# A two-layer encoder trunk on one core: token sums, unit order and conditioning products rearranged, and two of four weight sums formed by accumulating transfers

## The chip, the cores and the metric

The kernel runs on one core of a Trainium2 chip, in one launch. The metric is the device time of an execution in microseconds (us), lower is better: 1917.07 us in the median of three runs, 1916.01 to 1919.67. The engines are TensorE (PE; PEld is its weight load), VectorE (DVE), ScalarE (ACT), GpSimd (POOL) and SyncE (SP). Each runs its own instructions in the order of the program and waits for semaphores of the others. SP issues nearly all transfers, POOL a few.

## The reference

Two layers on x (512 tokens by 1024 channels), in float32, each a feed-forward half step, a mixer, and a second half step; the norms are scaled and shifted by m, which is a product of the conditioning vector c with w_mod:

```python
cond = jax.nn.silu(c)
for l in range(DEPTH):
    m = (cond @ w_mod[l] + b_mod[l]).reshape(bsz, 3, 3, D_MODEL)
    x = x + 0.5 * m[:, 0, 2][:, None] * swiglu(adaln_in(x, norm_g[l, 0], m, 0),
                                               ffn_w1[l, 0], ffn_w3[l, 0], ffn_w2[l, 0])
    h = adaln_in(x, norm_g[l, 1], m, 1) @ w_in[l]
    ...  # mixer: windowed attention and short convolution, or axial attention and Hyena
    x = x + m[:, 1, 2][:, None] * (mix @ w_out[l])
    x = x + 0.5 * m[:, 2, 2][:, None] * swiglu(adaln_in(x, norm_g[l, 2], m, 2),
                                               ffn_w1[l, 1], ffn_w3[l, 1], ffn_w2[l, 1])

def swiglu(h, w1, w3, w2):
    return (jax.nn.silu(h @ w1) * (h @ w3)) @ w2
```

D_FF is 2752, that is 21 hidden tiles of 128 and one of 64. The relative bias table (rel_table) enters the first layer's attention, and a filter computed from features, three small layers with sines and a Fourier transform enters the second layer's Hyena.

## The kernel before

**Products.** All data are float32. Each operand is split into a high and a low part (split, L203 on ScalarE copies the high part, L204 on VectorE subtracts), and a product is three matmuls of 128 by 128 weights: high by high, high by low, low by high (mm3, L224 to L226). Tokens stand in columns: 512 in one matmul, or two halves of 256.

**Feed-forward.** Each of the four runs over three groups of hidden tiles. In a group, the up part makes SwiGLU outputs into tiles ga, gb, gc, and then the projection (project, L358) makes eight output tiles dt from all of the group's tiles and adds them into x (L362). The weight of a projection's tile is w2a in the first group (8 loads of 384 KB) and w2b in the others (8 of 512 KB each). (0, 0), (0, 2), (1, 0), (1, 2) name the four by layer and place.

**Seven-product units.** In the first feed-forward tiles 5 to 20, in the others 2 to 20 are each a unit (up_seven): w1 and w3 over two halves of the channels and two halves of the tokens are taken as 2 by 2 blocks, and seven products of block sums replace eight (L477, 12 matmuls of 256 columns each, 84 in a unit). There are 73 units. The sums of tokens, T1 to T4, are made once for each feed-forward (token_sums, L409 to L421, from x, the norm's factor and a second pass of ScalarE at L412). The sums of weights are made in each unit by weight_sums: two loads of 512 KB on SP (raw1 and raw3), four VectorE operations of 512 columns (L454, L455, L457, L459) and splits into S1, S2, S3, S4, A11, A12, A22. The other tiles, which need no sums, are computed directly.

**Conditioning.** m is formed by 144 products (gemv): each is a 512 KB load of w_mod on SP (L240), one VectorE product with accumulation (L248), and a read of the accumulator. They are spread over the projections by a rate, so many for each output tile, as far ahead of their use as the rates put them.

**Bias and filter.** rel_bias (L1099, L1105) forms the bias of the first layer's attention by a small matmul, and repeats it through DRAM with a 2 MB transfer on POOL's queue. hyena_filter makes the filter: three matmuls with sines, eight matmuls (L965), a sum of squares (L978), its norm (L992), and a transform with matrices loaded on POOL's queue (dft_hi, dft_lo).

**Order.** The program is written as one sequence; a framework reorders each engine's instructions at build time by its own estimate, and tiles rotate through pools: 4 raw buffers, 5 each of wh and wl, 2 of e3, 16 of h, and 3 + 1 + 2 + 2 banks of PSUM. A load into a buffer is issued when the last reader of its former content is done. The order of a built program is fixed.

## Time and profile before

| | |
|---|---|
| profiled execution, whole | 1918.76 us |
| its span on the core | 1917.0 us |
| median of three runs | 1917.07 us |
| TensorE, VectorE, ScalarE, GpSimd busy | 1845.9, 1565.1, 1012.5, 3.6 us |
| moved by DMA, mean rate | 269.27 MB, 140 GB/s |

The span is the time from the first to the last instruction on the core, and 1.76 us lie around it. Busy times are sums over an engine's instructions; an engine can be busy and still be slowed, since a matmul's time is longer at a lower granted clock. The chain of work is followed back from the last instruction: at each step to what released it. A wait is idle time of an engine in front of an instruction, named after what ended it. The table of stretches gives for each stretch of the span the busy time of each engine, the granted clock of TensorE as a share of full speed, the share of time that the DMA engines worked, and the rate.

### The profile page before, as it was taken

The numbers are of one execution on the slowest core, as the hardware profiler recorded it, in microseconds if no ns is written. First come the engines' busy times: TensorE is split into PE (matmuls) and PEld (weight loads), VectorE is DVE, ScalarE is ACT, GpSimd is POOL, SyncE is SP. The second block draws the span as 40 slices with busy tenths as digits, with TensorE's granted clock in tenths as the row PEclk, the third lists the DMA queues.
The fourth block names the chain that finished last, engine by engine and source line by source line (L and its number), as shares of the span: only waits on it lengthen the run. The fifth ranks groups of instructions, "written<-read, shape, count | busy, mean of one in ns | idle before, by whom it ended". The sixth has DMA issues, their size and how long they took to land.

```text
span 1917.0 us, 30306 instructions
## 1 busy us (share of the span) xinstructions
PE 1845.9 (96%) x11844; PEld 1645.8 (86%) x11844; DVE 1565.1 (82%) x2681; ACT 1012.5 (53%) x1651; POOL 3.6 (0%) x9
## 2 busy tenths in 40 slices
PE   7889999999999999999989999998999999999999
PEld 5659889888888899798988989977887898898997
DVE  8989878878759898888899976877887889686682
ACT  5525435378848345254663533555788366353451
POOL 0000000000000000000000000000000000000000
PEclk9989999999999999999999999998999999999999
DMA  7664643842321644636427362344222322333231
GB/s 273 221 229 167 221 145 102 294 132 94 100 85 64 229 148 152 222 99 220 155 95 242 110 220 66 115 135 148 72 88 99 121 89 75 102 104 117 88 119 59
DMA packets 83658, 269.27 MB, mean 140 GB/s; under 512 B 10024, under 2 KB 13352, under 8 KB 83514
## 3 DMA queue, kind: packets, MB, share of 16 engines
q1 hardware_dynamic: 81898, 263.13, 41.0%
q0 software_dynamic: 1616, 4.20, 0.6%
q8 instruction: 93, 1.52, 0.3%
q14 instruction: 51, 0.42, 0.1%
HBM read 258.88 MB, written 10.50 MB: 141 GB/s over the span
## 4 chain that ended last, share of the span: by engine, by line
PE 73%; DVE 16%; DMA 6%; ACT 3%; issue 1%; SPq 0%; ACTq 0%; DVEq 0%
PE pA L477 29%; PE pC L358 18%; PE pV L477 5%; DVE wl L204 3%; PE pA L358 3%; DMA raw<-w2b 3%; DVE raw L248 2%; PE pC L225 2%; PE pC L226 2%; PE pC L224 2%; ACT wh L203 2%; DMA raw<-w2a 1%; DMA raw<-w_mod 1%; PE pA L789 1%; DVE h L345 1%
## 5 line engine op out<-in xcount | busy, mean ns | idle before, releaser
L203 ACT CAST wh<-raw 128x1024 fp32r<-128x1024 f32 (+2 forms) x393 | 372.8, 951 | 547.4 <-PE pA L477 194.6
L204 DVE TENSOR_TENSOR wl<-raw,wh 128x1024 fp32r<-128x1024 f32 (+2 forms) x393 | 432.1, 1102 | 120.3 <-ACT wh L203 117.1
L477 PE MATMUL pA<-h,wh 128*128 128x256 f32 x1752 | 331.2, 283 | 10.1 <-ACT h L203 9.2
L477 PE MATMUL pA<-e,wh 128*128 128x256 f32 x1752 | 333.4, 288 | 6.8 <-ACT tl L486 3.5
L477 PEld LDWEIGHTS pA<-e,wh 128*128 128x128 f32 x1752 | 271.5, 191 | 22.4 <-ACT tq L493 13.1
L477 PEld LDWEIGHTS pA<-h,wh 128*128 128x128 f32 x1752 | 275.7, 191 | 13.3 <-ACT h L203 9.9
L477 PE MATMUL pA<-e,wl 128*128 128x256 f32 x876 | 246.8, 282 | 0.0
L477 PE MATMUL pA<-h,wl 128*128 128x256 f32 x876 | 244.7, 283 | 1.9 <-DVE wl L204 1.9
L358 PE MATMUL pC<-gb,wh 128*128 128x512 f32 (+1 forms) x800 | 227.3, 368 | 3.6 <-ACT gb L203 1.6
L358 PE MATMUL pC<-ga,wh 128*128 128x512 f32 (+1 forms) x648 | 183.6, 371 | 5.0 <-DVE mod L261 2.6
L248 DVE SCALAR_TENSOR_TENSOR raw<-raw,cond 128x1024 f32<-128x1024 f32 x144 | 174.5, 1221 | 15.8 <-DMA raw<-w_mod 14.8
L358 PEld LDWEIGHTS pC<-gb,wh 128*128 128x128 f32 x800 | 143.9, 189 | 34.8 <-ACT gb L203 3.0
L477 PEld LDWEIGHTS pA<-h,wl 128*128 128x128 f32 x876 | 165.6, 189 | 2.3 <-DVE wl L204 2.3
L477 PEld LDWEIGHTS pA<-e,wl 128*128 128x128 f32 x876 | 167.4, 191 | 0.0
L358 PE MATMUL pC<-gb,wl 128*128 128x512 f32 (+1 forms) x392 | 143.8, 367 | 0.0
L358 PEld LDWEIGHTS pC<-ga,wh 128*128 128x128 f32 x648 | 115.5, 189 | 27.7 <-issue 3.9
L362 DVE SCALAR_TENSOR_TENSOR x<-pC,mod,x 128x512 f32<-128x512 f32 (+1 forms) x108 | 74.2, 687 | 74.7 <-PE pC L358 74.3
L358 PE MATMUL pC<-ga,wl 128*128 128x512 f32 (+1 forms) x300 | 111.6, 372 | 5.2 <-DVE wl L204 5.1
L203 ACT CAST wh<-e 128x1024 fp32r<-128x1024 f32 x73 | 76.8, 1052 | 60.6 <-PE pV L477 26.5
L477 PE MATMUL pV<-h,wh 128*128 128x256 f32 x584 | 107.1, 282 | 0.0
L225 PE MATMUL pA<-h,wh 128*128 128x256 f32 (+1 forms) x301 | 90.7, 310 | 2.1 <-DVE h L345 2.1
L477 PEld LDWEIGHTS pV<-h,wh 128*128 128x128 f32 x584 | 90.3, 190 | 0.0
(309 smaller groups left out, 3608.3 us busy)
## 6 DMA issues: line engine op xcount, KB each, us to landing
raw<-w SPq DMA_DIRECT2D x164, 512.0 KB, 3.5
raw<-w_mod SPq DMA_DIRECT2D x144, 512.0 KB, 4.5
raw<-w2b SPq DMA_DIRECT2D x64, 512.0 KB, 4.1
raw<-w_in SPq DMA_DIRECT2D x36, 512.0 KB, 4.5
raw<-w2a SPq DMA_DIRECT2D x32, 384.0 KB, 3.6
raw<-w_out SPq DMA_DIRECT2D x16, 512.0 KB, 3.4
raw<-w_start SPq DMA_DIRECT2D x8, 512.0 KB, 4.7
xs<-x SPq DMA_DIRECT2D x16, 256.0 KB, 2.0
```

Source lines behind the costliest of these rows:

```text
L203: self.nc.scalar.copy(out=hi, in_=src)
L204: self.nc.vector.tensor_sub(out=lo, in0=src, in1=hi.bitcast(F32))
L224: mm(out, lhsT=wh, rhs=rh, start=start, stop=False)
L225: mm(out, lhsT=wh, rhs=rl, start=False, stop=False)
L226: mm(out, lhsT=wl, rhs=rh, start=False, stop=stop)
L248: nc.vector.scalar_tensor_tensor(out=raw, in0=raw, scalar=1.0, in1=self.cond, op0=ALU.mult, op1=ALU.mult, accum_out=m[:, c : c + 1])
L345: nc.vector.tensor_sub(out=lo[:, c0:c1], in0=hf, in1=hi[:, c0:c1].bitcast(F32))
L358: nc.tensor.matmul(ps, lhsT=lh, rhs=r, start=q == 0, stop=q == len(todo) - 1)
L362: nc.vector.scalar_tensor_tensor(out=x, in0=ps, scalar=gate[dt], in1=x, op0=ALU.mult, op1=ALU.add)
L477: nc.tensor.matmul(out, lhsT=lh, rhs=rr, start=first and n == 0, stop=n == 11, skip_group_check=True)
L789: nc.tensor.transpose(tp[:, c * P : (c + 1) * P], pt[qb][:, o : o + P], self.ident)
```

## The change

- token_sums reads the parts h (high plus low, one addition of 512 columns per tile) and no longer x and the norm's factor. T1 and T2 have the opposite sign, and so has a unit's result, which the tail multiplies by -1. The split of T1 is put off to first_sum.
- In the first feed-forward, token_sums stands after tile 5 and first_sum after tile 7 of the second group, and tiles 5, 6, 7 are computed directly. 70 units are left.
- A unit's A22 and S4 products and its tail (finish) are issued after the next unit's A11 product. The first unit after the token sums has S4 and S1 exchanged (late_t1), and the tail of a group's last unit is done in two halves.
- Of the weight sums, a21 + a22 and a21 + a11 are formed by two transfers on POOL's queue that add 256 KB each into the target in SBUF (accum_op); the first goes into a tile s that a third load on SP of 256 KB fills. The other two stay on VectorE.
- The rates of the conditioning products change, and 24 are placed in units (in_up).
- rel_bias is called at the end of the third group in place of the second; the three small layers of the filter (filter_mlp) one group earlier.

```diff
--- before.py
+++ after.py
@@ -389,36 +389,33 @@
...
-    def token_sums(self, key):
-
+    def token_sums(self):
 
+        self.t1 = self.t("e3", (P, 1024))
         for j in range(4):
             f = []
             for kt in (j, j + 4):
-                a, b = self.ab[key + (kt,)]
-                xr = self.t("tq")
-                for c0, r in zip((0, HALF), self.rs):
-                    nc.vector.tensor_mul(
-                        out=xr[:, c0 : c0 + HALF], in0=self.x[kt][:, c0 : c0 + HALF], in1=r)
+                hi, lo = self.h[kt]
                 hf = self.t("th")
-                nc.scalar.activation(out=hf, in_=xr, func=AF.Identity, scale=a, bias=b)
+                nc.vector.tensor_add(out=hf, in0=hi.bitcast(F32), in1=lo.bitcast(F32))
                 f.append(hf)
             b11, b12 = f[0][:, :HALF], f[0][:, HALF:]
             b21, b22 = f[1][:, :HALF], f[1][:, HALF:]
-            s14, s23 = self.t("tq"), self.t("tq")
-            s1, s4, s2, s3 = s14[:, :HALF], s14[:, HALF:], s23[:, :HALF], s23[:, HALF:]
-            nc.vector.tensor_sub(out=s1, in0=b12, in1=b11)
-            nc.vector.tensor_sub(out=s2, in0=b22, in1=s1)
+            s4, s23 = self.t("tq")[:, :HALF], self.t("tq")
+            s1, s2, s3 = self.t1[:, j * HALF : (j + 1) * HALF], s23[:, :HALF], s23[:, HALF:]
+            nc.vector.tensor_sub(out=s1, in0=b11, in1=b12)
+            nc.vector.scalar_tensor_tensor(
+                out=s2, in0=s1, scalar=-1.0, in1=b22, op0=ALU.mult, op1=ALU.subtract)
             nc.vector.tensor_sub(out=s3, in0=b22, in1=b12)
-            nc.vector.tensor_sub(out=s4, in0=b21, in1=s2)
+            nc.vector.scalar_tensor_tensor(
+                out=s4, in0=s2, scalar=-1.0, in1=b21, op0=ALU.mult, op1=ALU.subtract)
...
-            self.split(s1, self.h[j][0][:, HALF:], self.h[j][1][:, HALF:])
...
+    def first_sum(self):
+
+        for j in range(4):
+            self.split(
+                self.t1[:, j * HALF : (j + 1) * HALF], self.h[j][0][:, HALF:], self.h[j][1][:, HALF:])
+
...
     def weight_sums(self, src1, src3):
 
+
         nc = self.nc
         raw1, raw3 = self.t("raw", (P, 1024)), self.t("raw", (P, 1024))
+        s = self.t("e3", (P, 1024))
+        a11, a12, a21 = raw1[:, :T], raw1[:, T:], raw3[:, :T]
         nc.sync.dma_start(out=raw1, in_=src1)
         nc.sync.dma_start(out=raw3, in_=src3)
-        s = self.t("e3", (P, 1024))
-        a11, a12, a21, a22 = raw1[:, :T], raw1[:, T:], raw3[:, :T], raw3[:, T:]
+        nc.sync.dma_start(out=s[:, :T], in_=src3[:, :T])
+        nc.gpsimd.dma_start(out=s[:, :T], in_=src3[:, T:], accum_op=ALU.add)
+        nc.gpsimd.dma_start(out=a21, in_=src1[:, :T], accum_op=ALU.add)
         x1 = self.split_new(raw1)
-        nc.vector.tensor_add(out=s[:, :T], in0=a21, in1=a22)
-        nc.vector.tensor_sub(out=s[:, T:], in0=s[:, :T], in1=a11)
+        cut = lambda pair, o: [v[:, o : o + T] for v in pair]
+        w = {"A11": cut(x1, 0), "A12": cut(x1, T)}
+        yield w
+        nc.vector.tensor_add(out=s[:, T:], in0=s[:, :T], in1=a11)
         x3 = self.split_new(s)
-        nc.vector.tensor_sub(out=a21, in0=a11, in1=a21)
         x2 = self.split_new(raw3)
-        nc.vector.tensor_sub(out=a12, in0=a12, in1=s[:, T:])
+        nc.vector.tensor_add(out=a12, in0=a12, in1=s[:, T:])
         x4 = self.split_new(a12)
...
-    def up_seven(self, src1, src3, gh, gl):
-
-        nc = self.nc
-        w = self.weight_sums(src1, src3)
-        q, p, r = self.ps("A")[:, :HALF], self.ps("V")[:, :HALF], self.ps("A")[:, :HALF]
-
...
+        w.update({"S1": cut(x3, 0), "S2": cut(x3, T), "S3": cut(x2, 0), "A22": cut(x2, T), "S4": x4})
+
...
+    def up_seven(self, src1, src3, gh, gl, before, late_t1=False, halves=False):
+        nc = self.nc
+        sums = self.weight_sums(src1, src3)
+        w = next(sums)
+        q, p = self.ps("A")[:, :HALF], self.ps("V")[:, :HALF]
...
-        product(q, "A11", "B11", True)
+        self.product(q, w["A11"], "B11", True)
         nc.scalar.copy(out=u1, in_=q)
-        product(p, "A12", "B21", True)
+        if before:
+            before()
+        next(sums, None)
+        r = self.ps("A")[:, :HALF]
+        self.product(p, w["A12"], "B21", True)
         nc.vector.tensor_add(out=sg[:, :HALF], in0=p, in1=u1)
-        product(q, "S2", "T2", False)
+        self.product(q, w["S2"], "T2", False)
         nc.scalar.copy(out=u2, in_=q)
-        product(r, "S1", "T1", True)
-        product(q, "S3", "T3", False)
+        if late_t1:
+            self.product(r, w["S4"], "B22", True)
+        else:
+            self.product(r, w["S1"], "T1", True)
+        self.product(q, w["S3"], "T3", False)
         nc.scalar.copy(out=c22, in_=q)
-        nc.vector.tensor_add(out=c22, in0=r, in1=c22)
-        product(q, "A22", "T4", False)
-        product(r, "S4", "B22", False)
-        nc.vector.tensor_add(out=sg[:, HALF:], in0=r, in1=u2)
-        nc.scalar.activation(out=sg, in_=sg, func=AF.Silu)
-        nc.vector.tensor_mul(out=sg[:, :HALF], in0=sg[:, :HALF], in1=q)
-        nc.vector.tensor_mul(out=sg[:, HALF:], in0=sg[:, HALF:], in1=c22)
-        self.split(sg, gh, gl)
+        nc.vector.tensor_tensor(out=c22, in0=c22, in1=r, op=ALU.subtract if late_t1 else ALU.add)
+
+        def finish():
+            self.product(q, w["A22"], "T4", False)
+            if late_t1:
+                self.product(r, w["S1"], "T1", False)
+                nc.vector.tensor_add(out=c22, in0=c22, in1=r)
+            else:
+                self.product(r, w["S4"], "B22", False)
+            neg = dict(scalar=-1.0, op0=ALU.mult, op1=ALU.mult)
+            if halves:
+                a, b = sg[:, :HALF], sg[:, HALF:]
+                nc.scalar.activation(out=a, in_=a, func=AF.Silu)
+                nc.vector.scalar_tensor_tensor(out=a, in0=q, in1=a, **neg)
+                self.split(a, gh[:, :HALF], gl[:, :HALF])
+                nc.vector.tensor_add(out=b, in0=r, in1=u2)
+                nc.scalar.activation(out=b, in_=b, func=AF.Silu)
+                nc.vector.scalar_tensor_tensor(out=b, in0=c22, in1=b, **neg)
+                self.split(b, gh[:, HALF:], gl[:, HALF:])
+                return
+            nc.vector.tensor_add(out=sg[:, HALF:], in0=r, in1=u2)
+            nc.scalar.activation(out=sg, in_=sg, func=AF.Silu)
+            nc.vector.scalar_tensor_tensor(out=sg[:, :HALF], in0=q, in1=sg[:, :HALF], **neg)
+            nc.vector.scalar_tensor_tensor(out=sg[:, HALF:], in0=c22, in1=sg[:, HALF:], **neg)
+            self.split(sg, gh, gl)
+
+        return finish
 
...
@@ -534,7 +568,8 @@
     def ffn(self, l, i, key, first=False):
         nc = self.nc
         k = 2 * l + (1 if i == 2 else 0)
-        rate = {(0, 0): (2, 2, 2), (0, 2): (2, 2, 2), (1, 0): (2, 1, 0), (1, 2): (0, 0, 0)}[l, i]
+        rate = {(0, 0): (1, 2, 2), (0, 2): (1, 2, 2), (1, 0): (1, 1, 0), (1, 2): (0, 0, 0)}[l, i]
+        in_up = {(0, 0): (2,), (1, 0): (1, 2)}.get((l, i), ())
         for g, fs in enumerate(GROUPS):
             new_g = self.g_tiles()
             gt = {}
...
...
+            pending = None
             for f in fs:
                 gt[f] = new_g()
+                if g in in_up:
+                    self.gemv(1)
                 if f == N_UP:
                     w = self.weight(self.up_unit(k, 2 * N_UP))
                     p = self.up_banks(1)[0]
@@ -592,20 +629,31 @@
                         self.mm3(p, self.block(w, kt), self.h[kt], kt == 0, kt == KT - 1)
                     self.glu(p[:64], p[64:], 64, *gt[f])
                     if not first:
-                        self.token_sums((l, i))
-                elif first and g == 0:
+                        self.token_sums()
+                        self.first_sum()
+                elif first and (g == 0 or f < 8):
                     ps = self.up_banks()
                     for s in range(2):
                         w = self.weight(self.up_unit(k, 2 * f + s))
                         for kt in range(KT):
                             self.mm3(ps[s], self.block(w, kt), self.h[kt], kt == 0, kt == KT - 1)
-                        self.gemv(4)
+                        if g == 0:
+                            self.gemv(4)
                     self.glu(ps[0], ps[1], P, *gt[f])
-                    self.token_sums((l, i))
+                    if f == 5:
+                        self.token_sums()
+                    if f == 7:
+                        self.first_sum()
                 else:
-                    self.up_seven(self.up_unit(k, 2 * f), self.up_unit(k, 2 * f + 1), *gt[f])
-            if (l, i, g) == (0, 0, 1):
+                    pending = self.up_seven(
+                        self.up_unit(k, 2 * f), self.up_unit(k, 2 * f + 1), *gt[f], pending,
+                        late_t1=f == (8 if first else 2), halves=f == fs[-1])
+            if pending:
+                pending()
+            if (l, i, g) == (0, 0, 2):
                 self.rel_bias()
+            if (l, i, g) == (1, 0, 1):
+                self.filter_mlp()
             if (l, i, g) == (1, 0, 2):
                 self.hyena_filter()
             rhs = []
@@ -931,25 +979,31 @@
-    def hyena_filter(self):
+    def filter_mlp(self):
...
         for s in range(3):
             p = self.ps("Q")[:64]
             nc.tensor.matmul(p, lhsT=lw[s], rhs=src, start=True, stop=True)
-            src = self.sin_tile(p, fc[:, 3:4], fc[:, 4 + s : 5 + s])
+            src = self.sin_tile(p, fc[:, 3:4], fc[:, 4 + s : 5 + s], "tq" if s < 2 else "rb")
+        self.fsrc = src
+
+    def hyena_filter(self):
+
+        nc, ap = self.nc, self.ap
+        src = self.fsrc
+        w4 = self.t("raw", (P, 1024))[:64]
+        nc.sync.dma_start(out=w4, in_=ap["f_w4"])
```

VectorE in the first feed-forward's first projection, before. L409 to L421 are the token sums, L248 the conditioning products, L362 the update of x by a projection's tile, wl the split of a w2a tile:

```order
L362 SCALAR_TENSOR_TENSOR x_66<-pC_843,mod_0_16_676,x_66 128x512
L418 TENSOR_TENSOR tq_822<-th_815 128x256
L420 TENSOR_TENSOR tq_823<-th_820,th_815 128x256
L419 TENSOR_TENSOR tq_823<-th_820,tq_822 128x256
L204 TENSOR_TENSOR h_142<-tq_822,h_141 128x256
L421 TENSOR_TENSOR tq_822<-th_820,tq_823 128x256
L248 SCALAR_TENSOR_TENSOR raw_866,mod_1_0_864<-raw_866,cond 128x1024
L204 TENSOR_TENSOR e_182_829<-tq_823,e_181_828 128x512
L204 TENSOR_TENSOR e_174_807<-tq_822,e_173_806 128x256
L204 TENSOR_TENSOR wl_871<-raw_869,wh_870 128x768
L248 SCALAR_TENSOR_TENSOR raw_895,mod_1_0_864<-raw_895,cond 128x1024
L625 CAST wh_870<-wl_871 64x128
```

The same place after: the update of x stands between splits and one conditioning product for each tile.

```order
L204 TENSOR_TENSOR wl_826<-raw_824,wh_825 128x768
L362 SCALAR_TENSOR_TENSOR x_66<-pC_743,mod_0_16_676,x_66 128x512
L673 CAST wh_825<-wl_826 64x128
L248 SCALAR_TENSOR_TENSOR raw_850,mod_1_0_764<-raw_850,cond 128x1024
L204 TENSOR_TENSOR wl_855<-raw_853,wh_854 128x768
L248 SCALAR_TENSOR_TENSOR raw_879,mod_1_0_764<-raw_879,cond 128x1024
L362 SCALAR_TENSOR_TENSOR x_67<-pC_773,mod_0_16_676,x_67 128x512
L673 CAST wh_854<-wl_855 64x128
L204 TENSOR_TENSOR wl_884<-raw_882,wh_883 128x768
```

What stood between them, the four rounds of token sums, is behind them now; and the number of L248 rows for an update has gone from two to one.

SP's queue in steady units, before (L449 and L450 are the loads of raw1 and raw3):

```order
L449 DMA raw_2698<-w 128x1024
L450 DMA raw_2699<-w 128x1024
L449 DMA raw_2826<-w 128x1024
L450 DMA raw_2827<-w 128x1024
```

The same queue after, in units of the first feed-forward's last group (L240 is the load of a conditioning weight, L454 and L455 those of raw1 and raw3, L456 the load of s):

```order
L240 DMA raw_2711<-w_mod 128x1024
L454 DMA raw_2714<-w 128x1024
L455 DMA raw_2715<-w 128x1024
L456 DMA e_497_2848<-w 128x512
L240 DMA raw_2843<-w_mod 128x1024
L454 DMA raw_2846<-w 128x1024
L455 DMA raw_2847<-w 128x1024
L456 DMA e_517_2980<-w 128x512
```

And POOL's queue there, where L457 adds into s and L458 into raw3's first half:

```order
L457 DMA e_477_2716<-w 128x512
L458 DMA raw_2715<-w 128x512
L457 DMA e_497_2848<-w 128x512
L458 DMA raw_2847<-w 128x512
```

A unit has two transfers on SP before; after, three and on POOL two, with one more on SP where a conditioning product stands in it.

TensorE where the Hyena filter ends, before: L358 is the projection after the last group of (1, 0), L965 a filter product, L992 the norm, L224 to L226 the transform.

```order
L358 MATMUL pC_13807<-gc_13145,wh_13738 128x256
L358 MATMUL pC_13807<-gc_13144,wl_13739 128x256
L965 MATMUL pQ_13406<-raw_13274,tq_13310 128x512
L965 MATMUL pQ_13413<-raw_13274,tq_13310 128x512
L992 MATMUL pQ_13431<-ones,acc_13322 128x2 x4
L224 MATMUL pQ_13449<-e_2285_13339,wh_13440 128x256
L225 MATMUL pQ_13449<-e_2286_13340,wh_13440 128x256
L226 MATMUL pQ_13449<-e_2285_13339,wl_13441 128x256
```

The filter's last products and the norm after, in the same projection:

```order
L358 MATMUL pC_13458<-gb_12851,wh_13453 128x512
L1019 MATMUL pQ_13238<-raw_13150,rb_11796 128x512
L1019 MATMUL pQ_13245<-raw_13150,rb_11796 128x512
L358 MATMUL pC_13458<-gb_12852,wh_13453 128x512
L358 MATMUL pC_13458<-gb_12851,wl_13454 128x512
L358 MATMUL pC_13458<-gc_12983,wh_13453 128x512
```

```order
L358 MATMUL pC_13528<-gb_12455,wl_13524 128x512
L1046 MATMUL pQ_13263<-ones,acc_13154 128x2 x4
L224 MATMUL pQ_13281<-e_2240_13171,wh_13272 128x256
L225 MATMUL pQ_13281<-e_2241_13172,wh_13272 128x256
L226 MATMUL pQ_13281<-e_2240_13171,wl_13273 128x256
L224 MATMUL pQ_13281<-e_2253_13199,wh_13272 128x256
L225 MATMUL pQ_13281<-e_2254_13200,wh_13272 128x256
```

The norm (L1046) and the transform stood right behind the last filter product; now the rows of 45 matmuls L358 lie between that product and the norm, and further L358 lie between parts of the transform. The first filter products stand ahead of this, inside the last unit.

## Rows read from the trace of the kernel before

**Rows 1.** The page: busy times, and the chain's shares by engine.

```profile
PE 1845.9 (96%) x11844; PEld 1645.8 (86%) x11844; DVE 1565.1 (82%) x2681; ACT 1012.5 (53%) x1651; POOL 3.6 (0%) x9
PE 73%; DVE 16%; DMA 6%; ACT 3%; issue 1%; SPq 0%; ACTq 0%; DVEq 0%
```

**Rows 2.** The chain, 227 to 280 us: start, length (us), engine, tile, line, count.

```profile
227.67 39.33 PE pC L358 x169
...
269.93 8.74 PE pA L477 x72
278.67 1.41 PE pV L477 x12
```

**Rows 3.** Table of stretches (see its header); the last three figures: clock, DMA share, GB/s.

```profile
core 0: us, PE busy (x) PEld busy (x) DVE busy (x) ACT busy (x) POOL busy (x), PEclk, DMA share, GB/s
20.00:58.00 38.00, 38.00 (x180) 32.22 (x181) 36.18 (x67) 19.72 (x25) 0.00 (x0) 1.00 0.85 298
...
83.00:136.00 53.00, 39.05 (x141) 26.16 (x139) 47.03 (x94) 15.95 (x24) 0.00 (x0) 0.87 0.62 206
...
267.00:328.00 61.00, 61.00 (x507) 59.84 (x506) 52.26 (x80) 33.67 (x52) 0.00 (x0) 1.00 0.28 93
...
585.00:621.00 36.00, 31.98 (x230) 29.57 (x229) 35.88 (x84) 29.67 (x53) 0.00 (x0) 0.96 0.09 30
...
1249.00:1301.00 52.00, 46.35 (x218) 33.53 (x218) 41.95 (x70) 28.96 (x40) 0.00 (x0) 0.96 0.34 116
```

**Rows 4.** TensorE's waits over the span: total us, times, longest.

```profile
PE pA L477 <- ACT h L203: 9.2, 3, 3.1
PE pQ L992 <- DVE acc L978: 5.7, 1, 5.7
PE pC L358 <- ACT gc L203: 5.4, 5, 1.8
...
PE pA L477 <- ACT tl L486: 3.5, 2, 2.4
...
PE pC L358 <- DVE gc L204: 2.4, 4, 0.6
...
PE pQ L224 <- ACT th L916: 2.1, 3, 0.7
```

**Rows 5.** Groups by line, 83 to 136 us: busy, mean ns | idle before.

```profile
L248 DVE SCALAR_TENSOR_TENSOR raw<-raw,cond 128x1024 f32<-128x1024 f32 x16 | 19.4, 1224 | 2.3 <-DMA raw<-w_mod 2.0
...
L1099 PE MATMUL pQ<-th,th 32*8 32x512 f32 x2 | 1.9, 1032 | 4.8 <-DMA th<-rel_hot 4.8
```

**Rows 6.** The chain, 80 to 137 us.

```profile
87.74 0.60 DVE gb L516
...
89.28 1.34 DVE tq L409 x4
...
104.15 6.31 DMA raw<-w2a
...
114.40 1.24 DVE raw L248 x2
...
125.67 4.52 DMA raw<-w2a
```

**Rows 7.** The chain, 139 to 151 us.

```profile
139.76 0.60 DVE raw L459
140.37 1.23 DVE wl L204
...
141.63 8.80 PE pA L477 x70
```

**Rows 8.** Transfers by queue: count, size of one, median us from issue to landing.

```profile
wl<-dft_lo POOLq DMA_DIRECT2D x2, 512.0 KB, 7.6
...
raw<-w_mod SPq DMA_DIRECT2D x144, 512.0 KB, 4.5
...
x<-xs SPq DMA_DIRECT2D x16, 256.0 KB, 2.7
```

29 lines of the change are left out of this document (11 added, 18 removed).

## The prediction

> **What bounds the kernel now.** I began with the busy times and the chain of work that ended last: TensorE is busy in 1845.9 of 1917.0 us and carries 73% of the chain, VectorE 16%, DMA 6% [rows 1]. So TensorE bounds it on the whole, and a change helps where TensorE waits or runs at a lower granted clock, not where VectorE merely gets less to do. The chain gives TensorE's spacing at full clock: 169 matmuls of 512 columns in 39.33 us, 0.2327 us each; and a seven-product unit, 72 + 12 matmuls of 256 columns, 8.74 + 1.41 = 10.15 us, with one unit right behind the other [rows 2].
>
> The table of stretches says where that holds. In steady units (267 to 328 us) TensorE is busy all 61.00 us although VectorE has 52.26: nothing is to be had there. Between 83 and 136 us, the projection after the first group of hidden tiles, it is busy for 39.05 of 53.00 us at a clock of 0.87, and VectorE for 47.03 [rows 3]. The waits name the rest: the projections' first pass waits for the last unit's output (gc, 5.4 + 2.4 us), a layer's first unit for the token sums (h on ScalarE L203, 9.2 us in three places), the Hyena filter for its sum of squares (acc L978, 5.7) and spectra (th L916, 2.1), and two unit ends for tl (3.5) [rows 4].
>
> **The change part by part.** The sum is made against the profiled execution, 1918.76 us; the runs' median, 1917.07, is 1.69 lower.
>
> *First projection.* At the spacing of [rows 2] its 136 matmuls take 136 x 0.2327 = 31.6 us; it has 53.0, so 21.4 are lost, two matmuls of rel_bias (1.9 us) among them [rows 3, 5]. In the chain VectorE's token sums come first (four L409 in 1.34 us, then differences and splits), then the conditioning products that stand behind them (L248, 1.24 us with its read), and each weight tile waits 4.5 to 6.3 us for w2a, whose buffer the backlog held [rows 6]. The change takes the token sums out of it (the first order fence) and halves the 16 L248: 8 x 1.22 = 9.8 us less there alone [rows 5]. The DMA left is 8 x (384 + 512) KB = 7.3 MB, 35.6 us at this stretch's 206 GB/s or 24.6 us at the 298 GB/s at which 20 to 58 us ran with TensorE wholly busy [rows 3]. I take the second, which is a stretch of the same mix, and leave 2.5 us for the first tiles: -18.9, and +1.9 since rel_bias' matmuls are done elsewhere, in the last unit of the third group, after a wait of 4.8 us for rel_hot [rows 5] that its loads, now issued a unit ahead, should hide: -17. By the first rate 4 us remain, so the bounds are -13 and -20.
>
> *Three direct tiles.* f = 5, 6, 7 of the first FFN are computed as 48 matmuls of 512 columns, 11.17 us, in place of 10.15: 3 x 1.02 = +3.1. The token sums, some 15 us of VectorE, lie beside them. The entry to the first unit, where TensorE now starts only at 141.6 us behind a VectorE sum and split of 0.60 + 1.23 us [rows 7], goes: -1.5 of these 1.8.
>
> *Pipelined units.* A22 and S4 with the SwiGLU tail go behind the next unit's A11, and a group's last unit has its tail in halves. In steady units there is nothing to gain, and nothing to lose while A11's split is early. At group ends a 256-column tail takes the place of a 512-column one, and A22's half is ready one product (1.41 us) sooner: about half of the 7.8 us of gc, -4. The tl waits follow VectorE's backlog of L248 behind the first projections, whose number is halved: -3 of 3.5. Bounds of both: 0 and -11.3.
>
> *Token sums of the other three FFNs.* Eight 512-wide additions (0.60 us each, as L516's row) replace sixteen 256-wide products (1.34 / 4 = 0.335) and eight ScalarE passes, so VectorE saves 5.4 - 4.8 = 0.6 us, and the two sums of each of the first two units, 4 x 0.60 = 2.4 us, leave as well [rows 6]. But in the new order the first unit's own split stands behind all token sums and first_sum. VectorE is back to back from 585 to 621 us (35.88 of 36) [rows 3]; some 3 us less of it, of which the first split feels about 1.3: 3 x 1.3 = -3.9. Bounds -10 (the wait gone) and +3.
>
> *Filter.* The three small matmuls move a group earlier, so the filter's products start inside the last unit, and 45 matmuls of L358, 10.5 us, lie between its last product and the norm that now waits 5.7 us; the DFT is spread among the projection (last order fence). 5.7 + 2.1 = 7.8, of which I take 6.5. The granted clock of 0.96 over 1249 to 1301 us [rows 3] is 2.1 us more that should come back: -2. Together -8.5, bounds -4 and -10.
>
> *Weight sums and accumulating transfers.* VectorE loses 2 x 0.60 us per unit of 52.26 / 61.00 x 10.15 = 8.7 [rows 2, 3, 6]: off the path, as it is idle for the rest of the 10.15. In their place come 140 transfers on the POOL queue and 70 loads on SP's, 768 KB a unit. The cover: in the new order s is reloaded once its buffer is free, 17 VectorE rows before its use at 13 rows a unit, 17 / 13 x 10.15 = 13.3 us; less 2.7 for the plain 256 KB load [rows 8], some 10 us are left for the accumulate. Where a unit also has a conditioning load, raw3's buffer comes round in two units, 20.3 us, and of these 4.5 go for that load, 1.2 for its product, at most as much as the first, 4.5, for raw3's load [rows 5, 8], and by the order some 4 in which the product stands behind other VectorE rows: about 6 us are left for a21. No row shows an accumulate. From below: a plain 256 KB load, 2.7 us. From above: 512 KB on the POOL queue, 7.6 us [rows 8], twice the bytes, as many as an accumulate moves if it also reads its target. The nearer row by size is the first, by queue the second; I take 5, between them, which both places hide, while 7.6 would stick out of the second by 1.6 us in up to 24 units, +38. As traffic a unit moves 1792 KB in 10.15 us, 181 GB/s, or 232 with a conditioning load; [rows 3] has 298. So 0, but without that cover each microsecond late costs 70 us over the 70 units.
>
> On the POOL queue's price the Trainium skill has a fit, "DMA: Bandwidth & Descriptors", section "Anatomy of one DMA — SWDGE (gpsimd) path": 2.0 us plus the bytes at 436 GB/s. That would be an estimated 2.6 us here and leave the sum as it is; the trace disagrees, since the fit makes 3.2 us of 512 KB where the row has 7.6. Against the change speaks "SBUF — State Buffer", section "SBUF: two separate sides": while VectorE runs an operation in a two-port mode such as a copy of 32-bit data, GpSimd can't write descriptors, and its transfer starves. In a unit VectorE has only operations on two tensors, and no run here shows such a starving; by that rule too the term stays 0 in units, and its failure is the first rival.
>
> Sum: -17 + 3.1 - 1.5 - 7 - 3.9 - 8.5 = -34.8, so 1918.76 - 34.8 = 1884.0, and against the median 1882.
>
> **Rivals.**
> *Accumulates late* (the other side). If the queue works them one after the other at over 5.08 us each, two don't fit into 10.15 us, and VectorE blocks in order at L463 and at raw3's split; behind these stand the next unit's A11 split and the tail, so TensorE stops in each unit. At 5.5 us a unit takes 11.0: 70 x 0.85 = +60, 1942. At 7.6 it would be 15.2 and far worse. For it: the 7.6 us of a plain transfer there, of as many bytes as an accumulate may move. Against: the program issues four such loads, 2 MB, one behind the other, so the landing may be mostly the sharing; and a queue need not be serial.
> *Startup bound by transfers.* At 206 GB/s and with the first w2a late as now (4.5 to 6.3 us [rows 6]) only half of the 17 is gained: 1891. For it: w2a's landings in the chain; against: 298 GB/s elsewhere.
> *Deferred work holds buffers.* wh and wl have five buffers, and a unit's A22 and S4 keep two of them into the next unit; then the next split waits and unit entries, group ends and token sums gain nothing: -17 + 3.1 - 1.5, and the filter, -8.5: 1893 by the median; at 0.2 us a unit more it is 1907.
> *All of it.* Every term at its better bound, -20 + 3.1 - 1.9 - 11.3 - 10 - 10 = -50: 1867.
>
> **How the numbers follow.** Forecast 0.42 (its own range 1870 to 1892), startup 0.20, buffers 0.12, all of it 0.12, late accumulates 0.14. Under 0.2%, about 3.8 us, no change can be told by a measurement. Slower is nearly all of the late accumulates, 0.13; same 0.04, from mild forms of these two; faster 0.83. The range for 8 in 10, 1865 to 1925, leaves out the worse part of the late accumulates and a little at the low end.
>
> **What would show it.** In the profile after: the first projection at 31 to 36 us with TensorE over 90% busy; no wait of L1046 on acc; the waits for h (L203) at the first units of the other three FFNs shorter by about 1.3 us each; unit after unit at 10.15 us with TensorE full; accumulates landing in 3 to 6 us. It is wrong if VectorE idles at L463 or L204 for a DMA into e3 or raw, and TensorE behind it; if the units' pieces in the chain exceed 10.2 us; or if POOL shows several microseconds per issue.

## The result and the profile after

The changed kernel takes 1968.13 us (median of four runs, 1958.28 to 1970.84) against 1916.54: ratio 1.0259, 95% interval 1.022 to 1.0297. It is slower by 2.6%, 51.6 us; I forecast 1882, 34.8 us faster, and 1968 lies outside my range. The profiled execution took 1967.23 us, its span 1965.4.

The page after, busy times and the chain's shares by engine, to be held against [rows 1]:

```profile
PE 1853.3 (94%) x11736; PEld 1656.6 (84%) x11736; DVE 1462.8 (74%) x2494; ACT 988.1 (50%) x1625; POOL 123.1 (6%) x149
...
PE 63%; DMA 16%; DVE 16%; ACT 3%; issue 2%; SPq 0%; DVEq 0%; ACTq 0%; POOLq 0%
```

VectorE does 102 us less, yet the chain goes through DMA for 16% of the span, not 6%. The table of stretches after (columns as in [rows 3]) shows where: the projection after the first group, then seven groups of hidden tiles, in the order (0, 0) third, (0, 2) second and third, (1, 0) second, (1, 0) third with the filter and its projection, (1, 2) second and third.

```profile
84.00:120.00 36.00, 33.31 (x137) 26.43 (x136) 33.65 (x60) 13.14 (x18) 0.00 (x0) 0.95 0.72 245
256.10:350.70 94.60, 85.28 (x676) 82.17 (x675) 70.50 (x112) 46.18 (x71) 10.18 (x12) 0.98 0.69 196
694.00:785.60 91.60, 84.19 (x676) 82.93 (x675) 62.59 (x97) 44.91 (x70) 11.08 (x13) 0.96 0.62 164
830.20:924.30 94.10, 85.34 (x676) 83.78 (x675) 64.00 (x100) 45.51 (x71) 9.38 (x11) 0.95 0.57 153
1074.10:1166.60 92.50, 85.36 (x679) 82.37 (x677) 69.06 (x108) 47.22 (x72) 11.09 (x13) 0.98 0.73 204
1212.80:1369.30 156.50, 150.26 (x1084) 137.01 (x1083) 114.58 (x186) 85.78 (x133) 11.54 (x15) 0.99 0.55 167
1698.00:1784.90 86.90, 82.74 (x676) 81.45 (x675) 58.97 (x91) 46.36 (x72) 11.09 (x13) 0.98 0.63 164
1828.60:1917.70 89.10, 81.86 (x676) 80.11 (x675) 58.96 (x90) 46.29 (x72) 9.37 (x11) 1.00 0.55 148
```

Some of the same stretches before: (0, 0) third, (0, 2) third, (1, 0) third with the filter, (1, 2) third.

```profile
266.80:348.60 81.80, 81.80 (x676) 80.16 (x676) 70.73 (x110) 44.70 (x69) 0.00 (x0) 1.00 0.37 123
...
811.40:893.10 81.70, 81.70 (x677) 80.10 (x676) 69.95 (x109) 44.74 (x69) 0.00 (x0) 1.00 0.38 122
...
1170.30:1333.80 163.50, 155.44 (x1090) 139.75 (x1089) 125.94 (x205) 87.01 (x135) 2.13 (x4) 0.97 0.34 115
...
1787.60:1869.30 81.70, 81.70 (x676) 80.06 (x675) 66.32 (x102) 45.82 (x70) 0.00 (x0) 1.00 0.34 109
```

The start does what was forecast: the first projection takes 36.0 us. But groups of units that TensorE filled for 97 to 100% before now take 87 to 95 us for the same 676 matmuls, with TensorE idle for up to 9 us of each and its clock at 0.95 to 1.00. VectorE's waits after (total us, times, longest) name what it stands at; L463 waiting for a transfer into e is one of the signs of being wrong that I had named:

```profile
DVE e L463 <- DMA e<-w: 77.2, 23, 6.5
...
DVE raw L248 <- DMA raw<-w_mod: 60.2, 36, 4.9
...
DVE e L463 <- DMA raw<-w: 18.8, 7, 4.5
```

TensorE's waits after show what that does to it: it waits for tc, VectorE's read of a PSUM bank (L529, L531), which stands behind the blocked L463 in VectorE's order, and for the splits (wl).

```profile
PE pA L477 <- DVE tc L529: 24.1, 18, 4.3
PE pA L477 <- DVE wl L204: 20.4, 4, 6.3
PE pA L477 <- DVE tc L531: 19.4, 7, 3.5
```

The new transfers after, by queue (count, size of one, median us from issue to landing); L457 and L458 are the two that add:

```profile
e<-w SPq DMA_DIRECT2D x70, 256.0 KB, 2.8
...
e<-w POOLq DMA_DIRECT2D x70, 256.0 KB, 5.3
...
raw<-w POOLq DMA_DIRECT2D x70, 256.0 KB, 4.3
```

So an accumulate lands in 5.3 us, close to the 5 that I took. Its length was right; its cover was not there. One turn of an s buffer in (1, 2), from the timeline after (start, length, engine, line; in brackets the idle time before):

```profile
1717.05 0.69 DVE L466 TENSOR_TENSOR raw<-raw,e 128x512 f32<-128x512 f32 x1
...
1717.80 0.33 SPq L456 DMA_DIRECT2D e<-w  x1
...
1721.16 0.84 POOL L457 DMA_DIRECT2D e<-w  x1 [5.63 <-DVE wl L204]
...
1726.99 0.69 DVE L463 TENSOR_TENSOR e<-e,raw 128x512 f32<-128x512 f32 x1 [5.43 <-DMA e<-w]
```

L466 of one unit is s's last reader; SP reloads the buffer 0.06 us after its end (1717.74), the accumulate follows at 1721.16 (its row names VectorE, but the load's landing, 2.8 us after its issue, is what came last), and L463 of the next unit but one can start at 1726.99: 9.25 us after the release, 5.43 of them with VectorE idle. The order of the program shows why. VectorE in (1, 2); in the trace this sequence stands at 1700.57 to 1712.24 us, one turn before the one above:

```order
L466 TENSOR_TENSOR raw_18560<-raw_18560,e_3244_18562 128x512
L500 TENSOR_TENSOR tc_18477<-pV_18474,tl_18475 128x256
L204 TENSOR_TENSOR wl_18622<-e_3244_18562,wh_18621 128x1024
L204 TENSOR_TENSOR wl_18626<-raw_18561,wh_18625 128x1024
L509 TENSOR_TENSOR tq_18476<-tq_18476,pA_18505 128x256
L204 TENSOR_TENSOR wl_18631<-raw_18560,wh_18630 128x512
L463 TENSOR_TENSOR e_3282_18820<-e_3282_18820,raw_18818 128x512
```

Here the split of s, the third row, is its last reader, and three rows lie between it and L463, the next use of the buffer (the last row). In the turn above L466 is the last reader, and four rows follow it, the last of which ends at 1721.56. In the trace, from a group's third unit on, groups with conditioning products have 15 to 18 such rows, mostly 17, which is where I had counted; (0, 2) and (1, 2) have 2 to 11.

### The profile page after: what moved, and what is told of

Same layout as the page of the kernel before. It is cut to its first block, busy times and chain, and to the rows that moved or that the text cites. A ratio compares the mean times of both kernels' runs of the same rounds, so it can differ in the third digit from the quotient of the medians.

```text
span 1965.4 us, 30550 instructions
## 1 busy us (share of the span) xinstructions
PE 1853.3 (94%) x11736; PEld 1656.6 (84%) x11736; DVE 1462.8 (74%) x2494; ACT 988.1 (50%) x1625; POOL 123.1 (6%) x149
## 4 chain that ended last, share of the span: by engine, by line
PE 63%; DMA 16%; DVE 16%; ACT 3%; issue 2%; SPq 0%; DVEq 0%; ACTq 0%; POOLq 0%
PE pC L358 18%; PE pA L477 17%; DMA raw<-w_mod 6%; DVE wl L204 5%; DMA e<-w 4%; PE pA L358 4%; DMA raw<-w2b 3%; DVE raw L248 3%; PE pV L477 2%; PE pC L225 2%; PE pC L224 2%; PE pC L226 2%; ACT wh L203 2%; PE pA L225 1%; PE pA L226 1%
## 5 line engine op out<-in xcount | busy, mean ns | idle before, releaser
L477 PE MATMUL pA<-h,wh 128*128 128x256 f32 x1680 | 322.5, 291 | 43.5 <-DVE tc L529 24.1
L477 PE MATMUL pA<-e,wh 128*128 128x256 f32 x1680 | 315.0, 285 | 11.3 <-ACT tl L502 6.1
L477 PEld LDWEIGHTS pA<-h,wh 128*128 128x128 f32 x1680 | 266.2, 195 | 51.9 <-DVE tc L529 27.9
L477 PEld LDWEIGHTS pA<-e,wh 128*128 128x128 f32 x1680 | 262.5, 193 | 18.1 <-ACT tq L508 10.2
L477 PE MATMUL pA<-e,wl 128*128 128x256 f32 x840 | 237.0, 282 | 0.0
L358 PE MATMUL pC<-gb,wh 128*128 128x512 f32 (+1 forms) x800 | 229.5, 371 | 5.0 <-ACT gb L549 2.4
L248 DVE SCALAR_TENSOR_TENSOR raw<-raw,cond 128x1024 f32<-128x1024 f32 x144 | 175.1, 1221 | 61.0 <-DMA raw<-w_mod 60.2
L358 PE MATMUL pC<-ga,wh 128*128 128x512 f32 (+1 forms) x648 | 183.4, 371 | 9.3 <-DVE x L362 6.7
L477 PEld LDWEIGHTS pA<-h,wl 128*128 128x128 f32 x840 | 163.5, 195 | 21.2 <-DVE wl L204 21.2
L358 PEld LDWEIGHTS pC<-gb,wh 128*128 128x128 f32 x800 | 145.7, 191 | 34.9 <-ACT gb L203 3.6
L477 PEld LDWEIGHTS pA<-e,wl 128*128 128x128 f32 x840 | 161.1, 192 | 0.0
L358 PEld LDWEIGHTS pC<-ga,wh 128*128 128x128 f32 x648 | 115.9, 189 | 34.4 <-issue 14.2
L358 PE MATMUL pC<-gb,wl 128*128 128x512 f32 (+1 forms) x392 | 144.6, 369 | 0.0
L458 POOL DMA_DIRECT2D raw<-w x70 | 60.0, 858 | 1260.1 <-DMA raw<-w 595.1
L362 DVE SCALAR_TENSOR_TENSOR x<-pC,mod,x 128x512 f32<-128x512 f32 (+1 forms) x108 | 74.1, 686 | 71.7 <-PE pC L358 71.2
L463 DVE TENSOR_TENSOR e<-e,raw 128x512 f32<-128x512 f32 x70 | 48.3, 689 | 96.2 <-DMA e<-w 77.2
L358 PE MATMUL pC<-ga,wl 128*128 128x512 f32 (+1 forms) x300 | 110.7, 369 | 0.0
L225 PE MATMUL pA<-h,wh 128*128 128x256 f32 (+1 forms) x333 | 103.1, 317 | 1.2 <-DVE h L345 1.2
```

What stands on the lines that cost most here:

```text
L225: mm(out, lhsT=wh, rhs=rl, start=False, stop=False)
L248: nc.vector.scalar_tensor_tensor(out=raw, in0=raw, scalar=1.0, in1=self.cond, op0=ALU.mult, op1=ALU.mult, accum_out=m[:, c : c + 1])
L358: nc.tensor.matmul(ps, lhsT=lh, rhs=r, start=q == 0, stop=q == len(todo) - 1)
L362: nc.vector.scalar_tensor_tensor(out=x, in0=ps, scalar=gate[dt], in1=x, op0=ALU.mult, op1=ALU.add)
L458: nc.gpsimd.dma_start(out=a21, in_=src1[:, :T], accum_op=ALU.add)
L463: nc.vector.tensor_add(out=s[:, T:], in0=s[:, :T], in1=a11)
```

## The experiments

Two theories were set against each other first. A: s's round trip (release, load, accumulate) is longer than the rows that VectorE has in between, and in groups with conditioning products raw's is as well. B, my third rival: the deferred A22 and S4 products hold wh and wl, whatever forms the sums. Some expectations add C: the 768 KB more that each unit moves cost by themselves. Ratios are to the kernel before, with 95% intervals; diffs are against the kernel after unless another is named.

**sums_on_vector.** All four weight sums on VectorE, nothing else undone.

```diff
-        nc.sync.dma_start(out=s[:, :T], in_=src3[:, :T])
-        nc.gpsimd.dma_start(out=s[:, :T], in_=src3[:, T:], accum_op=ALU.add)
-        nc.gpsimd.dma_start(out=a21, in_=src1[:, :T], accum_op=ALU.add)
...
+        nc.vector.tensor_add(out=s[:, :T], in0=a21, in1=raw3[:, T:])
         nc.vector.tensor_add(out=s[:, T:], in0=s[:, :T], in1=a11)
         x3 = self.split_new(s)
+        nc.vector.tensor_add(out=a21, in0=a11, in1=a21)
```

> The changed kernel with all four weight sums of a unit on VectorE again (same signs), no accumulating transfer and no third load on SP; all its other parts stay. Theory A (the accumulates' latency lies in two buffer rings that the static order gives too little slack): the eight-unit groups fall from 87 to 95 us to about 82, the third group's projection of the first FFN from 55.5 to 49, and the time to 1880 to 1895, as the sum of the prediction has it without its term on the accumulates. Rival B (the deferral of A22 and S4 stops the units, not the transfers): the groups stay over 86 us and the time over 1935.

1895.43 us, 0.9872 (0.9856 to 0.9887), just above the 1880 to 1895 that A expects; the projection of the third group, expected at 49 us, took 54.7 (bias_early takes this up). The accumulates cost 1968.1 - 1895.4 = 72.7 us, and the rest of the change gains 1.3%. Its table of stretches: first projection, the groups (0, 0) third, (0, 2) third, (1, 0) third with the filter, (1, 2) third.

```profile
83.50:119.60 36.10, 33.54 (x138) 26.66 (x137) 34.34 (x61) 12.52 (x17) 0.00 (x0) 0.95 0.72 247
248.00:333.00 85.00, 82.19 (x676) 79.88 (x675) 77.07 (x124) 46.07 (x71) 0.00 (x0) 1.00 0.50 157
...
805.00:885.70 80.70, 80.02 (x676) 79.57 (x675) 70.60 (x110) 45.72 (x71) 0.00 (x0) 1.00 0.37 119
...
1168.00:1315.20 147.20, 146.73 (x1083) 134.75 (x1082) 121.51 (x198) 85.42 (x133) 2.13 (x4) 1.00 0.44 147
...
1767.00:1847.00 80.00, 80.00 (x676) 79.67 (x676) 66.72 (x103) 46.59 (x72) 0.00 (x0) 1.00 0.35 111
```

The two other groups of (0, 2) and (1, 2) take 81.0 and 79.9 us, the second of (1, 0) 83.5. Over the seven groups shown of after the differences are 9.6, 10.6, 13.4, 9.0, 9.3, 7.0 and 9.1: 68 of the 70.7 us between the two spans. With the deferred products still in place, groups without conditioning products run at 80 to 81 us, so B falls.

**before_s_accumulates.** The kernel before, with only s formed by a load and an accumulate (in all of its 73 units; diff against before):

```diff
...
+        nc.sync.dma_start(out=s[:, :T], in_=src3[:, :T])
+        nc.gpsimd.dma_start(out=s[:, :T], in_=src3[:, T:], accum_op=ALU.add)
         x1 = self.split_new(raw1)
-        nc.vector.tensor_add(out=s[:, :T], in0=a21, in1=a22)
```

> The kernel before with one change: a21 + a22 of each of its 73 units by a plain load of s on SP and an accumulate on POOL's queue, in place of one VectorE addition; nothing is deferred or moved. In its order 3 to 15 rows of VectorE lie between the release of s's buffer and the sum that reads s. Theory A (buffer ring and order): the groups of eight units go from 82 to 86 up to 88 to 93 us, 1940 to 1965. Rival B (it takes the deferral of A22 and S4 for the transfers to hurt): 1914 to 1920.

1965.2 us, 1.0251 (1.023 to 1.0273). In the trace s's slack here is 2 to 14 rows from a group's third unit on, and one accumulate in each unit costs 47 us. VectorE stands 1.8 to 6.5 us at this sum where four rows lie in between, and at most 0.4 us where 14 do. Its VectorE wait and its transfer:

```profile
DVE e L456 <- DMA e<-w: 41.1, 17, 6.5
```

```profile
e<-w POOLq DMA_DIRECT2D x73, 256.0 KB, 5.6
```

There is no deferred work in this kernel, so B falls a second time.

**only_s_accumulates.** s as after; a21 + a11 back on VectorE.

```diff
-        nc.gpsimd.dma_start(out=a21, in_=src1[:, :T], accum_op=ALU.add)
...
         x3 = self.split_new(s)
+        nc.vector.tensor_add(out=a21, in0=a11, in1=a21)
```

> Only a21 + a22 is formed by an accumulate (with its load of s on SP); a21 + a11 is on VectorE. Theory A: raw3 is no longer held by an accumulate, so the groups with conditioning products in them (94.6 and 92.5 us) fall to about 83, while the groups without them (91.6, 94.1, 87.0, 89.1) keep most of their excess, since there VectorE waits at L463 for s: about 1925. Theory C (it is the traffic, 768 KB more a unit): two thirds of it are left, and every group keeps about two thirds of its excess: about 1940, with no difference between the two kinds of group.

1946.37 us, 1.0138 (1.0118 to 1.0158): 51 us more than sums_on_vector, so s is most of the cost. In total this is a miss, since I had expected about 1925. The groups part as A says, 86 us with conditioning products and 88 to 92 without; the stretches of (0, 0) third and (0, 2) second:

```profile
254.30:339.80 85.50, 83.25 (x675) 80.38 (x674) 72.83 (x117) 46.25 (x71) 4.28 (x5) 1.00 0.63 189
687.50:779.90 92.40, 84.58 (x661) 82.30 (x661) 67.49 (x107) 43.93 (x71) 5.96 (x7) 0.96 0.55 158
```

**only_a21_accumulates.** The other one alone.

```diff
-        nc.sync.dma_start(out=s[:, :T], in_=src3[:, :T])
-        nc.gpsimd.dma_start(out=s[:, :T], in_=src3[:, T:], accum_op=ALU.add)
-        nc.gpsimd.dma_start(out=a21, in_=src1[:, :T], accum_op=ALU.add)
...
+        nc.vector.tensor_add(out=s[:, :T], in0=a21, in1=raw3[:, T:])
+        nc.gpsimd.dma_start(out=a21, in_=src1[:, :T], accum_op=ALU.add)
```

> Only a21 + a11 is formed by an accumulate, and a21 + a22 on VectorE ahead of it, so the accumulate now also waits for VectorE's reading. Theory A: the groups without conditioning products lose the wait for s; but the accumulate stands behind a VectorE operation, so raw3 is ready at least 5 us after that; the groups with conditioning products keep their excess or grow. About 1930 to 1960. Theory C (traffic): one third is left, all groups fall alike, about 1910.

1900.24 us, 0.9901 (0.9885 to 0.9918). My expectation under A missed: alone, a21 costs about 5 us. Its group (0, 0) third takes 87.8 us, so each accumulate alone adds 0.5 to 2.8 us to that group, and the two together 9.6. That they add up to more than their sum is measured; why is not settled, but the place can be read: in this group VectorE waits at L248 for conditioning loads 3.9 us in sums_on_vector, 9.1 with s alone accumulated, 6.9 with a21 alone and 16.7 with both. The timeline of after shows the loop in that group, in which a raw buffer goes from raw3's split to a conditioning load and on to raw3's load:

```profile
302.61 1.23 DVE L204 TENSOR_TENSOR wl<-raw,wh 128x1024 fp32r<-128x1024 f32 x1
...
303.86 0.33 SPq L240 DMA_DIRECT2D raw<-w_mod  x1
...
309.19 1.22 DVE L248 SCALAR_TENSOR_TENSOR raw<-raw,cond 128x1024 f32<-128x1024 f32 x1 [3.01 <-DMA raw<-w_mod]
...
310.45 0.33 SPq L455 DMA_DIRECT2D raw<-w  x1
...
314.55 1.22 DVE L204 TENSOR_TENSOR wl<-raw,wh 128x1024 fp32r<-128x1024 f32 x1
```

The split ends, the conditioning load starts 0.02 us later, VectorE idles 3.01 us for it at L248, and the next unit's split stands behind that: 11.94 us from split to split, where a unit has 10.15.

**plain_transfers.** The two POOL transfers overwrite their targets in place of adding, so the two additions are left out.

```diff
-        nc.gpsimd.dma_start(out=s[:, :T], in_=src3[:, T:], accum_op=ALU.add)
-        nc.gpsimd.dma_start(out=a21, in_=src1[:, :T], accum_op=ALU.add)
+        nc.gpsimd.dma_start(out=s[:, :T], in_=src3[:, T:])
+        nc.gpsimd.dma_start(out=a21, in_=src1[:, :T])
```

> The changed kernel with the two transfers on POOL's queue as plain copies of the same rows into the same places with the same waits, so a21 + a22 and a21 + a11 are not added. If adding into SBUF is what makes them take 5.3 and 4.3 us, they land in 2.5 to 3.5 and the time falls by 20 to 40, 1930 to 1950. If the queue, its issue (0.86 us) and the load on the DMA engines make it, they land in 4 to 5 us and the time stays at 1955 to 1970.

1931.93 us, 1.0084 (1.0054 to 1.0113), halfway between after and sums_on_vector: 36 us of the 73 come from the adding, 37 are there for any transfers in these places. The time is the one expected if the adding makes the length; the landings are somewhat longer than the 2.5 to 3.5 expected then:

```profile
e<-w POOLq DMA_DIRECT2D x70, 256.0 KB, 3.9
raw<-w POOLq DMA_DIRECT2D x70, 256.0 KB, 3.3
```

**late_s_sum.** A copy of one column from the previous unit's S4 into s holds L463 back in VectorE's order, so that in the trace 12 to 23 rows lie between release and use from a group's third unit on (17 in steady units without conditioning products). The transfers are unchanged.

```diff
+        if self.last is not None:
+            nc.vector.tensor_copy(out=s[:, T : T + 1], in_=self.last[:, :1].bitcast(F32))
         nc.vector.tensor_add(out=s[:, T:], in0=s[:, :T], in1=a11)
...
+        self.last = x4[1]
...
```

> The changed kernel with both accumulates; a copy of one column from the low part of the last unit's S4 stands ahead of the VectorE sum that reads s (L463), so that the order holds this sum back behind that split: 16 to 20 rows of VectorE from the release of s's buffer to that sum in all units, in place of 3 to 12 in the groups without conditioning products. Theory A: these four groups (91.6, 94.1, 87.0, 89.1 us) fall to 82 to 84, the groups with conditioning products (94.6, 92.5) stay, and the time is about 1935 to 1945. Theory C (traffic, or the accumulates' duration alone): no group changes, 1968.

1929.19 us, 1.0053 (1.0038 to 1.0068), 39 us back. VectorE's wait for s, 77.2 us after, is nearly gone (L465 here is L463 of after):

```profile
DVE e L465 <- DMA e<-w: 1.0, 1, 1.0
```

The four groups without conditioning products in the table of after gain 39.5 us: 91.6, 94.1, 86.9 and 89.1 become 81.8, 80.5, 80.0 and 79.9. The second group of (0, 0), which also has none, falls from 91.8 to 87.2, and two projections of (0, 0) by some 5 us together; two groups with conditioning products ((0, 0) third and (1, 0) second) got worse by 3.8 and 7.1. Two of the four, and these two:

```profile
249.10:347.50 98.40, 88.42 (x676) 85.01 (x675) 72.53 (x118) 45.17 (x71) 10.16 (x12) 0.93 0.68 191
...
816.10:896.60 80.50, 80.27 (x677) 79.82 (x676) 63.13 (x103) 46.05 (x71) 9.39 (x11) 1.00 0.66 175
1046.80:1146.40 99.60, 89.36 (x679) 86.76 (x677) 72.50 (x121) 46.94 (x73) 11.08 (x13) 0.91 0.71 196
...
1801.10:1881.00 79.90, 79.90 (x677) 79.66 (x676) 60.05 (x97) 47.35 (x72) 9.38 (x11) 1.00 0.63 164
```

With all 140 accumulates at nearly the same lengths (5.2 and 4.5 us) and the same traffic, TensorE is full for 79.90 of 79.90 us: in these groups the slack decides, not the queue and not the bytes (C). Why the two groups with conditioning products got worse is open.

**late_sum_old_rates.** The same, and no conditioning products in units (the rates of before).

```diff
-        rate = {(0, 0): (1, 2, 2), (0, 2): (1, 2, 2), (1, 0): (1, 1, 0), (1, 2): (0, 0, 0)}[l, i]
-        in_up = {(0, 0): (2,), (1, 0): (1, 2)}.get((l, i), ())
+        rate = {(0, 0): (2, 2, 2), (0, 2): (2, 2, 2), (1, 0): (2, 1, 0), (1, 2): (0, 0, 0)}[l, i]
+        in_up = ()
```

> The kernel late_s_sum (both accumulates, L463 held back; 1929.2 us, its groups with conditioning products at 98.4 and 99.6 us) with the rates of conditioning products as in the kernel before and none in units. Theory A (an accumulate costs only where the order leaves it no slack; in the groups with conditioning products the ring of four raw buffers through w_mod, VectorE and raw3): all groups at 80 to 83 us, -30, and the first projection some 3 to 8 us longer with its 16 products: 1895 to 1908. Theory C (768 KB more a unit cost by themselves): those two groups stay over 88 us, 1915 or more.

1905.01 us, 0.994 (0.9921 to 0.9958), the time that A expects. (0, 0) third takes 82.3 us in place of 98.4; (1, 0) second takes 87.2 in place of 99.6, more than the 80 to 83 expected and than its 83.5 in sums_on_vector. So most of the accumulates' cost is hidden if s has its slack and no conditioning load shares raw with them; they still gain nothing over VectorE's sums.

**bias_early.** sums_on_vector, with rel_bias after the first group.

```diff
-            if (l, i, g) == (0, 0, 2):
+            if (l, i, g) == (0, 0, 0):
                 self.rel_bias()
```

> The kernel sums_on_vector (1895.4 us) with the call of rel_bias moved from the end of the third group of the first FFN to the end of the first, so that its 2 MB transfer runs beside units and no longer beside the third group's projection, its w2b and w_mod loads and the mixer. Theory D (that transfer and the late bias cost there: the projection takes 54.7 us in place of 48.6 before, the first mixer 142.6 in place of 137.0): both come back, -9 to -11, 1884 to 1887. Rival (the projection and the mixer lost that to the moved conditioning products or the order): both stay, 1893 to 1897.

1889.61 us, 0.9868 (0.9835 to 0.9901), the lowest median of all, though above the 1884 to 1887 of theory D. Against sums_on_vector the third projection of (0, 0) goes from 54.7 to 50.8 us and the mixer of layer 0 from 142.6 to 137.1; the first projection gives 3.7 back (36.1 to 39.8). By the ratios the two can't be told apart.

**bias_after_tile_6.** sums_on_vector, rel_bias between the direct tiles.

```diff
+                    if f == 6:
+                        self.rel_bias()
...
-            if (l, i, g) == (0, 0, 2):
-                self.rel_bias()
```

> The kernel sums_on_vector with rel_bias called after hidden tile 6 of the first FFN, behind the first projection: its matmul and loads are then out of that projection (which took 36.1 us in sums_on_vector, 39.8 in bias_early), and its 2 MB transfer runs beside units of the second group. Theory D (the bias costs by what its transfer and its late arrival stand beside): first projection 36, third group's projection 50 to 51, mixer 137: 1884 to 1887. Rival: the second group or its projection takes up what the others give, 1889 to 1895.

1890.2 us, 0.9865 (0.9842 to 0.9889), as the rival has it. First projection 36.5, third 49.8, mixer 137.0, but the second group takes 90.8 us where it took 84.7: the cost moves there.

**best.** bias_early, with first_sum behind the first unit of the other three FFNs.

```diff
-                        self.first_sum()
...
+                    if f == 2:
+                        self.first_sum()
```

> The kernel bias_early with the split of T1 (first_sum) called after the first unit of the other three FFNs instead of ahead of it, so that VectorE splits that unit's first weights without standing behind four more splits. TensorE waits there 6.5, 6.5 and 4.9 us in sums_on_vector. Theory: each shorter by 3 x 0.42 + what ScalarE's copies ahead of them take, 1.5 to 3 us, so 5 to 9 us below bias_early: 1876 to 1881. If the wait is for the token sums themselves, nothing changes against bias_early.

1895.59 us, 0.9891 (0.9866 to 0.9917): no gain where 5 to 9 us below bias_early were expected. At the first of these units TensorE's wait for the first split falls from 6.33 us in sums_on_vector to 2.58, but 2.56 and 0.76 us appear two products later, at S2.

**first_unit_by_transfer.** bias_after_tile_6 with first_sum as in best, and the sums of each first unit by the accumulates.

```diff
+        if by_dma:
...
-        sums = self.weight_sums(src1, src3)
+        sums = self.weight_sums(src1, src3, late_t1)
...
```

> The kernel bias_after_tile_6 with both sums of the one unit behind the token sums, in each FFN, formed by the two accumulating transfers (4 units of 70), where the order leaves them 120 rows of VectorE, and first_sum called after that unit in the three later FFNs. Theory A: these accumulates are hidden, VectorE has two operations (1.2 us) less there, and the unit waits 1.2 to 3 us less: 1877 to 1884. Rival (the wait there is set by the token sums ahead, and what is taken away is waited for one product later, as in the kernel best): no change, 1884 to 1888.

1890.92 us, 0.9874 (0.9848 to 0.9899): no difference to bias_after_tile_6.

## Why the prediction was wrong

The failed step is the accumulates at 0. I wrote that s is reloaded "17 VectorE rows before its use at 13 rows a unit, 17 / 13 x 10.15 = 13.3 us" and that this leaves "some 10 us" for the accumulate. The 17 rows hold in three groups; I counted there and took it for all; in their steady units the trace of after has 13.0 to 15.8 us from release to use, and the accumulate landed 2.5 to 6.3 us ahead of the use, so the working held where I had counted. With the four rows of the turn above the same working gives 4 / 13 x 10.15 = 3.1 us, against 9.25 measured for load and accumulate; the rows took 3.82 us, and 5.43 us of idle time make up the rest. before_s_accumulates and late_s_sum show it from both sides: short slack costs 47 us without the rest of the change, long slack gives 39 us back with all of it. My 5 us for one accumulate was right, and I even wrote what a lost cover costs ("each microsecond late costs 70 us"). The first rival named the place (L463, and raw3's split behind), the size (+60) and the sign, with a serial queue as its reason. The traces show no such queue: in late_s_sum POOL issued L457 at 1248.19 and L458 at 1250.14 us, they took 7.4 and 6.7 us and so landed 1.3 us apart, and with slack both fit into units of 10 us. I gave it 0.14, since I weighed the transfer's length, known within 2.7 to 7.6, and not the slack, which the order would have told exactly, group by group.

The second cover, raw3's in groups with conditioning products, "about 6 us", was wrong for the two accumulates together and nearly right for a21 alone (+5 us in all). In the loop above the conditioning load takes 5.3 us with its landing, for which I had 4.5, and VectorE's wait for it delays the split that frees the next buffer.

The other terms can be read from sums_on_vector (span 1894.7, 22.3 less than before), stretch by stretch from first to last matmul. Where a stretch is cut moves a row by some tenths; apart from the last row they add up to -21.4 of the 22.3:

| term | forecast, us | measured, us |
|---|---|---|
| first projection | -17 | -16.4 |
| direct tiles and entry | +1.6 | +0.5 |
| groups, their ends and tl | -7 | -8.8 |
| token sums of the other FFNs | -3.9 | +0.7 |
| (1, 0) third group, filter, projection | -8.5 | -16.1 |
| not in the sum: third projection of (0, 0), mixer of layer 0 | 0 | +6.0, +5.5 |
| not in the sum: first and third projection of (0, 2) | 0 | +3.0, +4.2 |
| accumulates (after against this run) | 0 | +72.7 |

- *First projection*: right, by the mechanism named (245 GB/s, TensorE busy for 33.3 of 36 us). The transfer-bound rival would have left half of the gain and falls.
- *Filter*: the right mechanism, forecast at half its size. The norm's wait for acc is gone from the rows of the waits; TensorE's idle time in this stretch fell from 163.5 - 155.4 = 8.1 to 0.5 us, close to the forecast. Its busy time fell by another 8.7, where I had allowed 2: 3.7 are the small matmuls (L951 before), which now stand a group earlier and which I had not priced, and the rest goes with the clock, from 0.97 to 1.00.
- *Token sums*: wrong. TensorE's wait at the first units has changed its name and grown; from the waits of sums_on_vector, where [rows 4] had h with 9.2:

```profile
PE pA L476 <- DVE wl L204: 17.8, 5, 6.3
```

  The first split stands behind more rows than I allowed for. best shows that taking first_sum away from it only moves the wait on to S2.
- *The bias*: a cost moved that I priced at nothing ("its loads, now issued a unit ahead, should hide"). Its 2 MB transfer and the products that need it now lie beside the w2b and w_mod loads of the third projection. TensorE there, in sums_on_vector, 337 to 395 us:

```profile
PE pC L358 <- DVE x L362: 6.1, 2, 3.9
```

  bias_early takes 3.9 us of this and 5.5 of the mixer's back, which shows the cause.
- The two projections of (0, 2) were 3.0 and 4.2 us longer in sums_on_vector, but only 0.4 and 1.2 us in bias_early, which has the same code there; their cause is open.

So without the accumulates the forecast's mechanisms gave about two thirds of the 34.8 us that I had added up, and the accumulates took it away three times over.

## What to carry to other kernels

A transfer in place of an engine's operation puts its issue and landing into the round trip of its buffer. Price that trip against the rows that the fixed order leaves between the last reader of a buffer and its next use, in every group and not at one place, and note that an engine off the path, VectorE here at 74%, stalls the bounding one as soon as it blocks in order ahead of a read that frees a PSUM bank. A bulk transfer or a small operation that is moved is priced where it lands as well as where it leaves.
